# First norm of a two-layer hybrid trunk: the modulation of two channel tiles stands ahead of the row sums, the row sums read one tile for two, and the reciprocal square root starts from one operation

## The chip, the cores and the metric

One core of a Trainium2 chip runs the whole program in one launch. The metric is the device time in microseconds (us) of a run. Matrix products run on TensorE (PE, with its weight loads PEld), elementwise work on VectorE (DVE), activations and casts on ScalarE (ACT), masks on GpSimd (POOL). SyncE (SP) only issues transfers. What a profile shows is one execution; the three timed runs of the kernel before gave 1694.21, 1692.0 and 1687.25 us.

## The reference

Two layers act on 256 latent tokens and 256 context tokens of 1024 channels. Only what matters for this change is shown: the first thing a layer does is an RMS norm over the channels of each token, scaled and shifted per channel by a modulation (adaLN) that is a product of the conditioning vector with a weight matrix; then one wide input projection feeds four mixers.

```python
def rmsnorm(x, g):
    y = xf * lax.rsqrt(jnp.mean(xf * xf, axis=-1, keepdims=True) + EPS)
    return y.astype(x.dtype) * g

def modulate(h, shift, scale):
    return h * (1 + scale) + shift

def trunk_layer(xs, cs, c, c_ctx, p, rope_ret, rope_mla, last):
    mod_x = jnp.split((jax.nn.silu(c) @ p['w_ada'] + p['b_ada'])[:, None, :], 6, axis=-1)
    mod_c = jnp.split((jax.nn.silu(c_ctx) @ p['w_ada'] + p['b_ada'])[None, None, :], 6, axis=-1)
    hx = modulate(rmsnorm(xs, p['norm1_g']), mod_x[0], mod_x[1])
    hc = modulate(rmsnorm(cs, p['norm1_g']), mod_c[0], mod_c[1])
    mx, mc = token_mixers(hx, hc, p, rope_ret, rope_mla, not last)
    ...
```

## The kernel before

Channels lie on the 128 partitions, tokens along the free axis. The 1024 channels are eight tiles of 128 (`KD`), and a tile holds 512 tokens: 256 latent, then 256 context (the two streams). Each fp32 operand of the large products is split into a rounded part (hi) and a rest (lo), and one product is three matmuls: hi with hi, hi with lo, lo with hi (`mm3`). The weights of the projections come as one stream of chunks of 128 x 1024 (`raw`); ACT casts a chunk to its rounded part (`whi`, L168), DVE subtracts to get the rest (`wlo`, L230, two instructions of 512 columns). Three chunks can be held split, six unsplit.

The head of the program, which the change touches, goes as follows. SP issues the eight tiles of x, then `first_load(u)`, four transfers of 256 KB with the modulation weights of channel tile u, mixed with chunks of the projection. ACT squares the tiles of x, and `sq_add` sums the squares on DVE; it always leaves the last tile apart, so two tiles remain. `tok_sums` sums over the partitions with matmuls against a column of ones, one per 128 tokens and per tile that remains. `rsqrt` makes a first guess from the bits of the number and refines it, in nine small DVE operations. `bcast` spreads the result over the partitions with four transposes. `first_mod(u)` makes the modulation of channel tile u: 16 matmuls of 32 x 128 against `cs` (the conditioning vectors; 32 passes in the trace), a copy by ACT, one small matmul against `halves` (two passes in the trace), and two small DVE operations that write `mod` and `moda`. `norm_apply` then makes the normed tile u: DVE scales it (L226), ACT adds the shift and rounds (hi, L163), DVE takes the rest (lo, L226). Then the 18 matmuls of tile u go into six accumulators (`pre`) that stay open over all eight tiles.

The program is written as a sequence of calls. A scheduler then puts each engine's instructions into one fixed row, by its own estimates and priorities (`tc.high_priority` moves a piece ahead); at run time an engine takes its row in order and waits on semaphores. Another call order at the head, or one operation fewer, thus also changes rows far from it. In the mixers of a layer an interleaver (`interleave`) also chooses between the projections and the mixers by running totals of each engine's estimated time (`clk`), to which each `ts` or `tt` adds.

`rsqrt` is called 17 times: at the first norm, in the mixers of both layers, at the later norms and at the final one.

Of the kernel before, what the change touches and what calls it, by code (L numbers as in the profile page):

```python
# [13 lines left out]
I32 = mybir.dt.int32  # L14
AF = mybir.ActivationFunctionType
ALU = mybir.AluOpType
# [3 lines left out]
KD = D // 128  # L20
# [131 lines left out]
def trunk(ctx: ExitStack, tc: tile.TileContext, xin: bass.AP, cin: bass.AP, par: bass.AP, con: bass.AP,  # L152
# [47 lines left out]
    U = Slots(upool, NSLOT)  # L200
# [4 lines left out]
    def nm(s):  # L205
        cnt[0] += 1
        return f"{s}_{cnt[0]}"

    def mm():
        return psm.tile([128, 512], F32, tag="mm", name=nm("mm"))  # L210

    def mx():
        return psx.tile([128, 512], F32, tag="mx", name=nm("mx"))

    def sm(shape, tag, dtype=F32, bufs=2):
        return small.tile(shape, dtype, tag=tag, name=nm(tag), bufs=bufs)

    def width(o):
        n_ = 1
        for d_ in o.shape[1:]:  # L220
            n_ *= d_
        return n_

    def stt(o, i0, s, i1, op0, op1):
        clk["dve"] += 65 + 1.17 * width(o)
        V.scalar_tensor_tensor(out=o, in0=i0, scalar=s, in1=i1, op0=op0, op1=op1)  # L226

    def tt(o, i0, i1, op):
        clk["dve"] += 65 + 1.1 * width(o)
        V.tensor_tensor(out=o, in0=i0, in1=i1, op=op)  # L230

    def red(o, i, op):
        clk["dve"] += 65 + 1.15 * width(i)
        V.tensor_reduce(out=o, in_=i, axis=AX.X, op=op)

    def ts(o, i0, s1, op0, s2=None, op1=None):
        clk["dve"] += 65 + 0.8 * width(o)
        if op1 is None:
            V.tensor_scalar(out=o, in0=i0, scalar1=s1, scalar2=None, op0=op0)
        else:  # L240
            V.tensor_scalar(out=o, in0=i0, scalar1=s1, scalar2=s2, op0=op0, op1=op1)  # L241

    MUL, ADD, SUB, MAX = ALU.mult, ALU.add, ALU.subtract, ALU.max
# [10 lines left out]
    def mm3(o, ah, al, bh, bl, start, stop):  # L254
        clk["pe"] += 1.26 * width(o)
        PE.matmul(o, ah, bh, start=start, stop=False, skip_group_check=True)
        PE.matmul(o, ah, bl, start=False, stop=False, skip_group_check=True)
        PE.matmul(o, al, bh, start=False, stop=stop, skip_group_check=True)
# [81 lines left out]
    def w_load(chunk):  # L340
        while W["dma"] <= min(chunk, NCHUNK - 1):
            t = wpool.tile([128, 1024], F32, tag="raw", name=nm("raw"), bufs=NRAW)
            nc.sync.dma_start(t, wst[W["dma"]])
            W["raw"][W["dma"]] = t
            W["dma"] += 1
# [24 lines left out]
    def w_block(b, n=1):  # L370
        w_ensure(b // 8)
        hi, lo = W["hl"][b // 8]
        o = (b % 8) * 128
        return hi[:, o:o + 128 * n], lo[:, o:o + 128 * n]
# [110 lines left out]

    def rsqrt(v, shape):

        y, s, ti = sm(shape, "rs_y"), sm(shape, "rs_s"), sm(shape, "rs_i", I32)
        with tc.high_priority():
            ts(ti, v.bitcast(I32), 1, ALU.logical_shift_right)  # L490
            ts(y.bitcast(I32), ti, -1, MUL, 0x5F3759DF, ADD)

            tt(s, y, y, MUL)
            tt(s, s, v, MUL)
            stt(s, s, -10.0 / 3, s, ADD, MUL)
            stt(y, s, 5.0, y, ADD, MUL)
            stt(s, y, -0.5 * 0.375 ** 3, y, MUL, MUL)
            tt(s, s, v, MUL)
            stt(y, s, 1.5 * 0.375, y, ADD, MUL)
        return y  # L500

    def tok_sums(sums, N):

        nb = N // 128
        p = mx()
        for i, tiles in enumerate(sums):
            for b in range(nb):
                for j, t in enumerate(tiles):
                    PE.matmul(p[:, i * nb + b:i * nb + b + 1], t[:, b * 128:(b + 1) * 128], one, start=j == 0,
                              stop=j == len(tiles) - 1, skip_group_check=True)  # L510
        return p[:, 0:len(sums) * nb].rearrange("p (i b) -> p i b", b=nb)

    def rstd_of(sums, N, n, merge=True):
        shape = [128, len(sums), N // 128]
        if merge:
            r = sm(shape, "toks")
            for i, tiles in enumerate(sums):
                if len(tiles) == 2:
                    t = tiles.pop()
                    tt(tiles[0][:, :N], tiles[0][:, :N], t[:, :N], ADD)  # L520
                    U.put(t)
                p = mx()
                for b in range(N // 128):
                    PE.transpose(p[:, b * 128:(b + 1) * 128], tiles[0][:, b * 128:(b + 1) * 128], ident)
                red(r[:, i, :], p[:, :N].rearrange("p (b t) -> p b t", t=128), ADD)
            ts(r, r, 1.0 / n, MUL, EPS, ADD)
            return rsqrt(r, shape)
        r = sm(shape, "toks")
        ts(r, tok_sums(sums, N), 1.0 / n, MUL, EPS, ADD)
        return rsqrt(r, shape)  # L530

    def bcast(r, N):

        p = mx()
        for b in range(N // 128):
            PE.transpose(p[:, b * 128:(b + 1) * 128], r[:, b:b + 1].to_broadcast([128, 128]), ident)
        return p

    def sq_add(acc, src, N):

        t = U([128, N])
        A.activation(t[:, :N], src, AF.Square)
        acc = acc or []
        if len(acc) < 2:
            return acc + [t]
        tt(acc[0][:, :N], acc[0][:, :N], acc[1][:, :N], ADD)
        U.put(acc[1])
        return [acc[0], t]
# [13 lines left out]
    def norm_apply(hx, src, s, rb, ab, only=None, r0=0):  # L562

        c = slice(s * SEQ, (s + 1) * SEQ)
        for k in range(KD) if only is None else [only]:
            y = U([128, SEQ])
            hi, lo = hx[k]
            b = ab[1][:, k, s:s + 1]
            stt(y, src[k][:, c], ab[0][:, k, s:s + 1], rb[:, r0:r0 + SEQ], MUL, MUL)
            A.activation(hi[:, c], y, AF.Identity, bias=b)  # L570
            stt(lo[:, c], y, b, hi[:, c].bitcast(F32), ADD, SUB)
            U.put(y)
# [47 lines left out]
    def first_load(u):  # L620
        if u < KD:
            ada_tiles[u] = [U([128, 512]) for _ in range(4)]
            for i_, t_ in enumerate(ada_tiles[u]):
                nc.sync.dma_start(t_, wfirst[u, i_])
# [3 lines left out]
    def first_mod(u):  # L628

        p = mx()  # L630
        for k in range(KD):
            for h in range(2):
                j = h + 2 * (k % 2)
                PE.matmul(p[32 * j:32 * j + 32, 0:128], cs[:, k, :],
                          ada_tiles[u][k // 2][:, (2 * (k % 2) + h) * 128:(2 * (k % 2) + h + 1) * 128], start=k < 2,
                          stop=k >= KD - 2, tile_position=(0, 32 * j), skip_group_check=True)
        U.put(ada_tiles.pop(u))
        sb = U([128, 128])
        A.copy(sb, p[:, 0:128])
        PE.matmul(p[:, 128:132], sb, halves, start=True, stop=True, skip_group_check=True)  # L640
        U.put(sb)
        o = PCOL["bada"][0]
        with tc.high_priority():
            tt(mods[0][:, u:u + 9:8, :], p[:, 128:132].rearrange("p (h s) -> p h s", h=2),
               params[0][:, o + u:o + u + 9:8].unsqueeze(2).to_broadcast([128, 2, 2]), ADD)
            stt(moda[:, u, :], mods[0][:, 8 + u, :], 1.0,
                params[0][:, PCOL["n1g"][0] + u:PCOL["n1g"][0] + u + 1].to_broadcast([128, 2]), ADD, MUL)
# [3 lines left out]
    first_load(1)  # L651
    w_load(1)
    first_load(2)
    nc.sync.dma_start(cons[:, nfirst:], con[:, nfirst:nres])
    acc = None
    for k in range(KD):
        acc = sq_add(acc, xs[k], T)
    rs = rstd_of([acc], T, D, False)
    U.put(acc)
    rb = bcast(rs[:, 0, :], T)  # L660
    hx = [None] * KD
    pre = [mm() for _ in range(4)] + [mx() for _ in range(2)]
    pos = w_take([(("w_in", 0), k, cols) for k in range(KD)
                  for cols in [misc_cols] + [ar(OFF["xbc"] + 128 * c) for c in FIRST]])
    W["ahead"], W["load"] = 0, 1
    began = clk["pe"]
    first_mod(0)
    for u in range(KD):
        hx[u] = U.pair(T)
        for s in range(2):  # L670
            norm_apply(hx, xs, s, rb, (moda, mods[0][:, 0:8, :]), u, s * SEQ)
        if u + 1 < KD:
            first_mod(u + 1)
        for i, ps in enumerate(pre):
            wh, wl = w_block(pos + 6 * u + i)
            mm3(ps, wh, wl, hx[u][0], hx[u][1], u == 0, u == KD - 1)
        first_load(u + 3)
    W["ahead"], W["load"] = AHEAD, NLOAD
    U.put(xs)
    for c0 in range(2048, 6144, 1024):  # L680
# [2 lines left out]
    for l in range(L):  # L683
# [817 lines left out]
        if last:  # L1501
            acc = r
# [11 lines left out]
    for b in range(2):  # L1514
        for h in range(2):
            p, y = mm(), U([128, 512])
# [132 lines left out]
```

## Time and profile before

| | |
|---|---|
| median of three runs | 1692.0 us (1687.25 to 1694.21) |
| the profiled execution's own time | 1692.55 us |
| its span on the core | 1690.8 us |
| PE busy | 1641.8 us, 97% of the span |
| DVE busy | 1312.9 us, 78% |
| ACT busy | 812.0 us, 48% |
| bytes moved | 259.04 MB, 153 GB/s over the span |

Busy shares are means over stages with different limits. PE's matmuls are pipelined, so its busy time also holds time in which it is slowed by its clock or by weight loads. Times of rows are counted from the start of the span.

### The profile page before, as it was taken

What the parts mean: (1) busy time and instruction counts of PE and PEld (TensorE: products, weight loads), DVE (VectorE), ACT (ScalarE), POOL (GpSimd) and SP (SyncE); (2) the same over time, 40 slices, a digit from 0 to 9 for tenths busy, and PEclk for the clock granted to TensorE, in tenths of its full rate; (3) what the DMA queues carried; (4) which work ended last, traced back from release to release, by engine and by line L of the source; (5) the groups of instructions that cost most, each with busy time, mean ns of one, the idle gap of its engine ahead of it and who ended that gap; (6) DMA issues with size and microseconds to landing.
All of it is one profiled execution on the core that took longest, in us unless ns stands there. A gap on an engine that the chain in (4) does not pass through costs nothing.

```text
span 1690.8 us, 24270 instructions
## 1 busy us (share of the span) xinstructions
PE 1641.8 (97%) x8926; PEld 1359.7 (80%) x8926; DVE 1312.9 (78%) x2676; ACT 812.0 (48%) x1378; POOL 53.5 (3%) x89
## 2 busy tenths in 40 slices
PE   6999999999999999999999999999999999999998
PEld 4777766778888888988888889978778788778887
DVE  4779999988578568887666757699889967887765
ACT  3475759462234233522212235457577545455654
POOL 0020200000000000000000000001110000000000
PEclk9999999999999999999999999999999999999999
DMA  9353321214445445465456646445433377646664
GB/s 362 122 145 113 114 68 54 75 38 131 157 126 185 130 157 187 128 196 165 148 174 190 228 146 203 143 126 164 123 100 101 100 221 244 211 152 189 185 188 141
DMA packets 85096, 259.04 MB, mean 153 GB/s; under 512 B 9648, under 2 KB 18784, under 8 KB 84976
## 3 DMA queue, kind: packets, MB, share of 16 engines
q1 hardware_dynamic: 73584, 244.15, 45.8%
q10 hardware_dynamic: 10624, 12.28, 2.9%
q0 software_dynamic: 768, 1.05, 0.3%
q8 instruction: 70, 1.15, 0.3%
q14 instruction: 50, 0.41, 0.1%
HBM read 253.70 MB, written 2.18 MB: 151 GB/s over the span
## 4 chain that ended last, share of the span: by engine, by line
PE 86%; DVE 5%; DMA 4%; ACT 3%; issue 1%; POOL 0%; ACTq 0%; DVEq 0%; SPq 0%
PE mm L187 74%; PE mx L187 9%; DMA u<-drow 3%; PE mx L191 2%; DVE u L226 2%; ACT u L163 2%; DVE wlo L230 1%; DVE u L230 1%; ACT whi L168 1%; ACT u L168 1%; DVE u L241 0%; DMA u<-u 0%; DMA u<-xin 0%; DMA raw<-w_ada 0%; DMA drow<-u 0%
## 5 line engine op out<-in xcount | busy, mean ns | idle before, releaser
L187 PE MATMUL mm<-u,whi 128*128 128x512 f32 (+1 forms) x4088 | 1149.6, 362 | 3.7 <-DVE u L226 1.8
L187 PEld LDWEIGHTS mm<-u,whi 128*128 128x128 f32 x4088 | 728.1, 189 | 130.5 <-issue 12.1
L187 PE MATMUL mm<-u,wlo 128*128 128x256 f32 (+1 forms) x2332 | 785.3, 337 | 0.0
L168 ACT CAST whi<-raw 128x1024 fp32r<-128x1024 f32 x351 | 368.4, 1050 | 548.7 <-PE mm L187 328.8
L230 DVE TENSOR_TENSOR wlo<-raw,whi 128x512 fp32r<-128x512 f32 x702 | 461.7, 688 | 165.7 <-ACT whi L168 164.4
L187 PEld LDWEIGHTS mm<-u,wlo 128*128 128x128 f32 x2332 | 441.8, 189 | 47.0 <-issue 2.0
L226 DVE SCALAR_TENSOR_TENSOR u<-raw,cs,u 128x512 f32<-128x512 f32 x210 | 148.2, 746 | 80.7 <-DMA raw<-w_ada 80.6
L163 ACT ACTIVATE u<-u 128x256 f32<-128x256 f32 (+5 forms) x262 | 122.7, 484 | 150.5 <-DVE u L230 105.8
L187 PE MATMUL mm<-whi,u 128*128 128x512 f32 x544 | 172.7, 394 | 0.5 <-ACT u L163 0.5
L230 DVE TENSOR_TENSOR u<-u,u 128x256 f32<-128x256 f32 (+5 forms) x290 | 160.3, 571 | 8.3 <-ACT u L163 3.2
L187 PE MATMUL mx<-u,u 128*64 128x256 f32 (+6 forms) x644 | 132.1, 396 | 12.3 <-ACT whi L168 3.8
L226 DVE SCALAR_TENSOR_TENSOR u<-u,convw,u 128x510 f32<-128x510 f32 (+29 forms) x240 | 134.0, 599 | 0.0
L187 PEld LDWEIGHTS mx<-u,u 128*64 128x64 f32 (+3 forms) x644 | 79.8, 165 | 54.3 <-issue 13.5
L187 PEld LDWEIGHTS mm<-whi,u 128*128 128x128 f32 x544 | 101.8, 188 | 23.3 <-issue 1.7
L187 PE MATMUL mm<-wlo,u 128*128 128x512 f32 x272 | 106.4, 391 | 0.0
L163 ACT ACTIVATE u<-mm 128x512 f32<-128x512 f32 (+3 forms) x110 | 60.6, 553 | 40.1 <-PE mm L187 35.7
L226 DVE SCALAR_TENSOR_TENSOR u<-u,mm 128x512 f32<-128x512 f32 (+1 forms) x94 | 60.0, 647 | 19.8 <-PE mm L187 18.2
L226 DVE SCALAR_TENSOR_TENSOR u<-u,u 128x256 fp32r<-128x256 f32 (+3 forms) x113 | 61.0, 550 | 10.3 <-ACT u L163 10.3
L187 PEld LDWEIGHTS mm<-wlo,u 128*128 128x128 f32 x272 | 51.1, 188 | 10.7 <-issue 0.4
L168 ACT COPY u<-mx 128x512 f32<-128x512 f32 (+4 forms) x82 | 38.5, 495 | 38.1 <-PE mx L187 36.4
L191 PE MATMUL mx<-cons,u 128*128 128x128 f32 (+1 forms) x292 | 44.1, 276 | 4.8 <-DVE u L230 3.1
L1056 POOL TENSOR_SCALAR_AFFINE_SELECT u<-u 128x256 f32<-128x256 f32 x24 | 17.4, 726 | 983.2 <-DVE u L241 825.5
(116 smaller groups left out, 890.3 us busy)
## 6 DMA issues: line engine op xcount, KB each, us to landing
raw<-wst SPq DMA_DIRECT2D x354, 512.0 KB, 3.7
raw<-w_ada SPq DMA_DIRECT2D x72, 512.0 KB, 4.1
u<-wfirst SPq DMA_DIRECT2D x32, 256.0 KB, 6.0
u<-drow ACTq DMA_DIRECT2D x32, 256.0 KB, 4.7
u<-xin SPq DMA_DIRECT2D x16, 256.0 KB, 4.3
u<-w_ada SPq DMA_DIRECT2D x16, 256.0 KB, 5.3
u<-drow ACTq DMA_DIRECT2D x16, 128.0 KB, 3.9
spill<-u SPq DMA_DIRECT2D x8, 128.0 KB, 3.6
```

Source lines behind the costliest of these rows:

```text
L163: nc.scalar.activation(o, *a, **k)
L168: nc.scalar.copy(o, i)
L187: PE._place(nc.tensor.matmul(*a, **k))
L191: PE._place(nc.tensor.transpose(*a, **k))
L226: V.scalar_tensor_tensor(out=o, in0=i0, scalar=s, in1=i1, op0=op0, op1=op1)
L230: V.tensor_tensor(out=o, in0=i0, in1=i1, op=op)
L1056: G.affine_select(out=a_[:, 0:4:3], in_=a_[:, 0:4:3], pattern=[[0, 2], [1, 128]], compare_op=ALU.is_ge, fill=-1e5, base=0, channel_multipl ...
```

## The change

Three edits. `rsqrt` makes its first guess in one DVE operation: the integer bits are multiplied by -0.5 and the magic constant is added, where there had been a shift and then a multiply by -1 with the addition. At the first norm the two remaining tiles of squares are added by DVE, so that the ones matmuls read one tile. And the modulation runs ahead: `first_mod(0)` stands before that addition and the sums, `first_mod(1)` behind the broadcast, and in the loop `first_mod(u + 2)` stands behind the matmuls of tile u, where `first_mod(u + 1)` had stood before them; the loads are issued one tile earlier to match.

```diff
     def rsqrt(v, shape):
 
-        y, s, ti = sm(shape, "rs_y"), sm(shape, "rs_s"), sm(shape, "rs_i", I32)
+        y, s = sm(shape, "rs_y"), sm(shape, "rs_s")
         with tc.high_priority():
-            ts(ti, v.bitcast(I32), 1, ALU.logical_shift_right)
-            ts(y.bitcast(I32), ti, -1, MUL, 0x5F3759DF, ADD)
+            ts(y.bitcast(I32), v.bitcast(I32), -0.5, MUL, 0x5F3759DF, ADD)
...
     first_load(2)
+    first_load(3)
     nc.sync.dma_start(cons[:, nfirst:], con[:, nfirst:nres])
     acc = None
     for k in range(KD):
         acc = sq_add(acc, xs[k], T)
+    first_mod(0)
+    tt(acc[0], acc[0], acc[1], ADD)
+    U.put(acc.pop())
     rs = rstd_of([acc], T, D, False)
     U.put(acc)
     rb = bcast(rs[:, 0, :], T)
+    first_mod(1)
...
     began = clk["pe"]
-    first_mod(0)
     for u in range(KD):
         hx[u] = U.pair(T)
         for s in range(2):
             norm_apply(hx, xs, s, rb, (moda, mods[0][:, 0:8, :]), u, s * SEQ)
-        if u + 1 < KD:
-            first_mod(u + 1)
         for i, ps in enumerate(pre):
             wh, wl = w_block(pos + 6 * u + i)
             mm3(ps, wh, wl, hx[u][0], hx[u][1], u == 0, u == KD - 1)
-        first_load(u + 3)
+        if u + 2 < KD:
+            first_mod(u + 2)
+        first_load(u + 4)
```

Place 1, the start of PE's row. `one` marks the row sums, `rs_y` the broadcast, `cs` the modulation matmuls (a row of four is a quarter of a tile's modulation), `cons` with size 128x4 the small matmul against `halves`, `mm_` and `whi` the projection. Before, where `mx_203` is the modulation of tile 0 and `mx_235` that of tile 1:

```order
L187 MATMUL mx_170<-one,u_147 128x1
L187 MATMUL mx_170<-one,u_166 128x1
L191 MATMUL mx_192<-cons,rs_y_180 128x128 x4
L187 MATMUL mx_203<-u_118,cs 32x128 x4
L187 MATMUL mx_203<-u_119,cs 32x128 x4
L187 MATMUL mx_203<-u_120,cs 32x128 x4
L187 MATMUL mx_203<-u_121,cs 32x128 x4
L187 MATMUL mx_235<-u_128,cs 32x128 x4
L187 MATMUL mx_203<-cons,u_220 128x4
```

The same place of the changed kernel, with `mx_177` for tile 0, `mx_222` for tile 1 and `u_250` for the first normed tile:

```order
L187 MATMUL mx_177<-u_118,cs 32x128 x4
L187 MATMUL mx_177<-u_119,cs 32x128 x4
L187 MATMUL mx_201<-one,u_155 128x1 x4
L187 MATMUL mx_177<-u_120,cs 32x128 x4
L187 MATMUL mx_177<-u_121,cs 32x128 x4
L191 MATMUL mx_217<-cons,rs_y_207 128x128 x2
L187 MATMUL mx_177<-cons,u_194 128x4
L191 MATMUL mx_217<-cons,rs_y_207 128x128 x2
L187 MATMUL mx_222<-u_128,cs 32x128 x4
L187 MATMUL mx_222<-u_129,cs 32x128 x4
L187 MATMUL mm_244<-u_250,whi_260 128x512
```

The modulation of tile 0 moved ahead of the sums (one half) and under the reciprocal root (the other half); the second half of tile 1's, which stood wholly ahead of the first projection matmul, now stands among those.

Place 2, in PE's row, where the modulation of channel tile 4 is made. Before (`mx_428`), at the border of two tiles, with `u_418` and `u_419` the hi and lo of the next one:

```order
L187 MATMUL mx_428<-u_345,cs 32x128 x4
L187 MATMUL mx_428<-u_346,cs 32x128 x4
L187 MATMUL mx_428<-u_347,cs 32x128 x4
L187 MATMUL mx_428<-u_348,cs 32x128 x4
L187 MATMUL mm_197<-u_418,whi_399 128x512
L187 MATMUL mm_197<-u_419,whi_399 128x512
L187 MATMUL mx_428<-cons,u_445 128x4
L187 MATMUL mm_197<-u_418,wlo_400 128x512
```

In the changed kernel (`mx_413` is tile 4, `mx_471` tile 5), inside tile 2's matmuls:

```order
L187 MATMUL mx_413<-u_308,cs 32x128 x4
L187 MATMUL mx_413<-cons,u_430 128x4
L187 MATMUL mx_471<-u_370,cs 32x128 x3
L187 MATMUL mx_248<-u_378,whi_402 128x512
L187 MATMUL mx_248<-u_379,whi_402 128x512
L187 MATMUL mx_249<-u_378,whi_402 128x512
L187 MATMUL mx_249<-u_379,whi_402 128x512
L187 MATMUL mx_248<-u_378,wlo_403 128x512
L187 MATMUL mx_249<-u_378,wlo_403 128x512
```

The small matmul now stands directly behind the modulation that feeds it through ACT, with no projection matmul between. On ACT the cast of `whi_402` stands directly behind the copy for that small matmul, and on DVE `wlo_403` stands behind the small operations of tile 4 and its two scalings.

Place 3, in DVE's row, at the modulation of tile 7 (`mx_608` before, `mx_593` after). Before:

```order
L226 SCALAR_TENSOR_TENSOR u_599<-u_604,mod_115,u_598 128x256
L230 TENSOR_TENSOR wlo_645<-raw_579,whi_644 128x512 x2
L230 TENSOR_TENSOR wlo_841<-raw_642,whi_840 128x512 x2
L230 TENSOR_TENSOR mod_115<-mx_608,par_99 128x2x2
L226 SCALAR_TENSOR_TENSOR moda_117<-mod_115,par_99 128x2
L226 SCALAR_TENSOR_TENSOR u_657<-u_93,moda_117,mx_192 128x256
L226 SCALAR_TENSOR_TENSOR u_661<-u_93,moda_117,mx_192 128x256
```

In the changed kernel (`u_617` and `u_621` scale the two streams of tile 6, `u_652` and `u_656` those of tile 7):

```order
L226 SCALAR_TENSOR_TENSOR u_617<-u_91,moda_117,mx_217 128x256
L230 TENSOR_TENSOR wlo_640<-raw_574,whi_639 128x512 x2
L226 SCALAR_TENSOR_TENSOR u_616<-u_617,mod_115,u_615 128x256
L230 TENSOR_TENSOR wlo_836<-raw_637,whi_835 128x512 x2
L230 TENSOR_TENSOR mod_115<-mx_593,par_99 128x2x2
L226 SCALAR_TENSOR_TENSOR u_621<-u_91,moda_117,mx_217 128x256
L226 SCALAR_TENSOR_TENSOR moda_117<-mod_115,par_99 128x2
L226 SCALAR_TENSOR_TENSOR u_652<-u_93,moda_117,mx_217 128x256
```

The scaling of tile 6's second stream moved behind the operation that waits for tile 7's modulation; in PE's row the first projection matmul of tile 6 stands right behind that modulation and its small matmul.

## Rows read from the trace of the kernel before

**Rows 1.** The page: engines' busy time, and the chain that ended last.
```profile
PE 1641.8 (97%) x8926; PEld 1359.7 (80%) x8926; DVE 1312.9 (78%) x2676; ACT 812.0 (48%) x1378; POOL 53.5 (3%) x89
...
PE 86%; DVE 5%; DMA 4%; ACT 3%; issue 1%; POOL 0%; ACTq 0%; DVEq 0%; SPq 0%
```

**Rows 2.** Busy time by stretch: PE, PEld, DVE, ACT, POOL, clock, DMA share, GB/s.
```profile
0.00:30.70 30.70, 13.86 (x106) 11.67 (x106) 13.41 (x48) 10.91 (x22) 0.77 (x9) 0.94 0.96 349
30.70:75.00 44.30, 44.30 (x364) 34.62 (x363) 28.54 (x67) 19.00 (x34) 0.00 (x0) 1.00 0.57 202
```

**Rows 3.** Timeline of PE, 13 to 25 us: start, duration, instruction, idle before.
```profile
13.07 3.55 PE L187 MATMUL mx<-one,u 128*128 128x1 f32 x16 [13.07 <-DVE u L230]
18.66 1.11 PE L191 MATMUL mx<-cons,rs_y 128*128 128x128 f32 x4 [2.04 <-DVE rs_y L226]
...
24.79 0.66 PE L187 MATMUL mm<-u,whi 128*128 128x512 f32 x1 [1.59 <-ACT u L163]
```

**Rows 4.** Timeline of the head, DVE.
```profile
12.23 0.69 DVE L230 TENSOR_TENSOR u<-u,u 128x512 f32<-128x512 f32 x1
...
16.66 0.16 DVE L241 TENSOR_SCALAR toks<-mx 128x4 f32<-128x4 f32 x1 [3.73 <-PE mx L187]
16.85 0.17 DVE L239 TENSOR_SCALAR rs_i<-toks 128x4 int32<-128x4 int32 x1
...
22.52 0.68 DVE L230 TENSOR_TENSOR wlo<-raw,whi 128x512 fp32r<-128x512 f32 x1
...
23.31 0.87 DVE L226 SCALAR_TENSOR_TENSOR u<-u,moda,mx 128x256 f32<-128x256 f32 x2
```

**Rows 5.** Issues of tile 0's modulation weights; landing times, issues of 0 to 60 us.
```profile
6.76 2.36 SPq L624 DMA_DIRECT2D u<-wfirst  x4
...
u<-wfirst SPq DMA_DIRECT2D x32, 256.0 KB, 6.0
raw<-wst SPq DMA_DIRECT2D x12, 512.0 KB, 6.6
```

**Rows 6.** Timeline at the border of channel tiles 0 and 1; a later chunk's split.
```profile
30.60 0.39 PE L187 MATMUL mx<-u,wlo 128*128 128x512 f32 x1
30.92 0.81 PEld L187 LDWEIGHTS mx<-u,cs 128*32 128x32 f32 x32 [0.35 <-issue]
...
31.93 0.73 PE L187 MATMUL mm<-u,whi 128*128 128x512 f32 x2
32.07 0.27 ACT L168 COPY u<-mx 128x128 f32<-128x128 f32 x1 [4.55 <-PE mx L187]
32.38 0.31 PEld L187 LDWEIGHTS mx<-cons,u 128*128 128x128 f32 x2 [0.16 <-ACT u L168]
...
32.64 0.48 PE L187 MATMUL mm<-u,wlo 128*128 128x512 f32 x1
...
33.21 0.87 DVE L226 SCALAR_TENSOR_TENSOR u<-u,moda,mx 128x256 f32<-128x256 f32 x2
...
37.78 1.05 ACT L168 CAST whi<-raw 128x1024 fp32r<-128x1024 f32 x1
...
39.55 1.29 DVE L230 TENSOR_TENSOR wlo<-raw,whi 128x512 fp32r<-128x512 f32 x2
```

**Rows 7.** Chain that ended last: start, duration, piece: ten projection matmuls.
```profile
32.78 2.40 PE mm L187 x10
```

**Rows 8.** Busy time and clock of one microsecond after the first projection matmul.
```profile
25.00:26.00 1.00, 1.00 (x4) 0.98 (x4) 0.51 (x3) 0.83 (x1) 0.00 (x0) 0.50 1.04 399
```

**Rows 9.** PE's waits for the reciprocal root: total, times, longest; and the last root.
```profile
PE mx L191 <- DVE rs_y L226: 6.0, 7, 2.0
...
1683.00 0.18 DVE rs_i L239
```

**Rows 10.** The longest wait of PE behind the head, and its stretch.
```profile
1203.76 1.08 PE L187 MATMUL mx<-u,u 128*64 128x256 f32 x2 [3.83 <-ACT whi L168]
...
1200.00:1210.00 10.00, 6.24 (x17) 4.51 (x18) 8.19 (x19) 4.77 (x11) 3.33 (x3) 0.66 0.29 103
```

## Prediction

> **What bounds the kernel now.** I read the page first: PE is busy 97% of the span, and 86% of the chain that ended last lies on it [rows 1]. So a change pays where PE waits or where its work gets shorter. The table by stretches shows one large place: in the first 30.7 us PE is busy only 13.9, and from 30.7 to 75 us it has no idle time at all [rows 2]. The head is therefore where a wait can go, and behind it anything put between PE's matmuls costs its full time. The timeline of the head shows the chain: the last sum of squares on DVE starts at 12.23, the ones matmuls run from 13.07, DVE reads their result at 16.66, the broadcast starts at 18.66, the first normed tile is scaled at 23.31 and the first projection matmul starts at 24.79 [rows 3, 4].
>
> **What the change removes, at the first matmul.** One more addition of 0.69 us on DVE [rows 4] puts the sums to 13.76. Half of 16 passes go, at 3.55 / 16 = 0.222 each [rows 3]: 1.78 us. One operation of the root goes; its step is 16.85 - 16.66 = 0.19 [rows 4]. The broadcast then starts at 18.66 + 0.69 - 1.78 - 0.19 = 17.38. It takes 1.11 [rows 3]. The small matmul of tile 0 stands inside it and costs what it costs at a tile border: from 31.93 to 32.64 PE does two projection matmuls and it [rows 6], and ten projection matmuls take 2.40, so 0.24 each [rows 7]; 0.71 - 0.48 = 0.23. The broadcast is done at 18.72, where it had been done at 19.77. Before, the scaling came 3.54 us behind it: the modulation of tile 0, its copy, its two small operations, and half a weight split of 0.68 at 22.52 [rows 4] stood between. Now the modulation runs ahead of the sums and under the root, and the split stands behind the scaling, so the scaling starts at about 18.75. That is 4.56 us earlier, and the first projection matmul comes at 20.23 instead of 24.79.
>
> The transfers allow it. The four issues of tile 0's weights end at 9.12, and a landing takes 6.0 in the median: 15.1 at the latest, before the sums end at 13.76 + 1.78 = 15.5 [rows 5]; half of them aren't waited for by the sums at all. The chunk that tile 2 first needs is now issued behind four more transfers. With it, 8 x 256 KB of x, 20 x 256 KB of modulation weights, 832 KB of constants, 3 x 512 KB of the projection and some 0.4 MB of parameters have to come, about 10.2 MB, which at the head's 349 GB/s [rows 2] is 29 us; a landing of such a chunk takes 6.6 in the median [rows 5], most of it the same queueing. By the sums below, tile 2 needs it after 33 us. I cost the changed order of SP at 0; if that cover were gone, it would cost the 3 us that the extra 1 MB takes, once.
>
> **What PE pays back, up to its 75th microsecond.** Three terms.
>
> (a) The modulation matmuls lie less well. A whole group of 32 passes lies between the matmul at 30.60 and the one at 31.93 [rows 6]: 1.33 - 0.24 = 1.09, of which 0.81 are its weight loads, 0.025 per pass, and 0.28 the change of shape in and out. Before, tile 1's group ran while PE waited, and six groups lay between projection matmuls. Now half of tile 1's passes lie there too, 16 x 0.025 = 0.40. Tile 1's second half lies in two pieces, tile 2's group in three, tile 5's in two (one of them at tile 4's), so there are ten changes of shape instead of six: 4 x 0.28 = 1.12. Sum 1.5; from 0.4, if a change of shape costs nothing among these, to 2.3, if the first two pieces run at the half clock and take twice as long.
>
> (b) At tile 4's modulation the small matmul stands directly behind it. Take T for PE's next free slot, 31.93 in the rows. The copy runs from T + 0.14 to T + 0.41, and PE is past the small matmul at T + 0.71 [rows 6]; before, projection matmuls covered that and it cost 0.23. Behind it ACT casts the chunk which the next matmuls need, 1.05 [rows 6], to T + 1.46. Behind the scaling, which starts at T + 1.28 and takes 0.87, DVE splits it, in two halves of 0.65 [rows 6], to T + 2.80 or T + 3.44. PE does a piece of tile 5 and four matmuls meanwhile, 0.23 + 0.38 + 0.96 = 1.57 without a wait, and then needs that split: it loses 1.2, or 1.9 if it needs both halves. I take 1.2, since the next block lies in the first half; 0 if tile 2 already lags behind.
>
> (c) At tile 7's modulation the second stream of tile 6 is scaled only behind the operation that waits for tile 7's small matmul. The scaling starts at T + 1.28 less one small step, T + 1.1, and takes 0.44 for one stream. From the scaling at 23.31 to the first matmul at 24.79 it took 1.48 with two streams [rows 3, 4], so 0.61 beyond them. PE goes on at T + 2.1 instead of T + 0.23: 1.9. It is 0 only if an engine did not keep to its row.
>
> On (b) and (c) the rows of before show what a row's order means: the load for the small matmul waits 0.16 at 32.38, and the projection matmul behind it, whose data had long been there, starts only at 32.64 [rows 6]. The Trainium skill ("TensorE: Matmul & The Clock Gate", Part 2) states that "the MATMULs themselves stay in program order" and that only weight loads are pulled ahead. By that rule (b) and (c) are paid in full; were it otherwise, the sum would be that of the second rival.
>
> The head thus gains 4.56 and pays 1.5 + 1.2 + 1.9 = 4.6: nothing is left, 0.0.
>
> **The other sixteen roots.** The last one lies bare at the end, its first operation at 1683.00 [rows 9]: 0.19. PE waited for a root seven times, 6.0 in all, 2.04 of them at the first [rows 3, 9]; the other six can lose 0.19 each, 1.1, or nothing where DVE does other work between the steps. I take 0.5.
>
> **Sum.** 1692.55, the profiled execution's own time, 0.0 for the head, - 0.2, - 0.5: 1691.85. That execution stands 0.55 above the median of the runs, so 1691.3. Bounds: with nothing paid back and all six waits shortened, 1692.0 - 4.56 - 0.2 - 1.1 = 1686.1; with the upper ends 2.3 + 1.9 + 1.9 = 6.1 and no shorter wait, 1692.0 + 1.5 - 0.2 = 1693.3.
>
> **Rivals.**
>
> First, the clock. Tile 0 took from 24.79 to 30.84, 6.05 us, where 18 matmuls and a small one are 4.56 [rows 3, 6, 7]: 1.5 lost, while PE ran at a granted 0.50 (1.2 GHz), having waited 1.59 just before [rows 3, 8]. If PE, with less waiting ahead of tile 0, keeps 2.4 GHz there, the time is 1689.8. For it: PE now works through most of 13.7 to 19.5. Against: it still waits some 0.9 before the first matmul, for the scaling and its rounding. The same page, Part 1, says that the window of this gate is free-running and doesn't reset at a kernel's start; by that the 1.5 would come and go from run to run in both kernels. No row of one execution shows it.
>
> Second, the early start is kept: the pieces hide in waits, and the engines' real times at (b) and (c) leave no wait. 1692.0 - 4.56 - 0.7 = 1686.7. For it: DVE and ACT have much idle time from 30.7 to 75 us [rows 2]. Against: their rows are fixed, and the waits follow from the rows, not from load.
>
> Third, slower: a new wait in a mixer. The scheduler put PE's, ACT's and DVE's rows of both layers' mixers in another order at many places. Where a cast of weights comes to stand on ACT behind an operation that waits for a transfer, PE runs out of split weights. The longest such wait of before is 3.83 us, and its stretch of 10 us ran at 0.66 of the clock [rows 10], so 6.8 us at half speed and at most 3.4 lost besides: 7.2. One more of these gives 1698.5. It decides as soon as it is over 0.7, and needs ACT to wait longer than the split chunks held ahead last. For it: such waits are there. Against: the interleaver's totals moved by only some 0.07 us per root, and most rows moved by a few places.
>
> Fourth, the same reordering takes that wait away: 1684.1.
>
> That the change does not do what it says, I can exclude for the order: the rows show it.
>
> **How the numbers follow.** Forecast, 45%: 1691.3, its own range 1688.5 to 1694. Clock 10%, 1689.8. Early start kept 20%, 1686.7. New wait 14%, 1698.5 or, with two, beyond 1700. A wait gone 11%, 1684.1 or, with the early start kept, below 1683. The range 1684.5 to 1698.5 leaves out half of each of the last two cases and a little of the rest. 0.5%, 8.5 us, is about what a measurement of this kernel can tell from no change: that is below 1683.5 or above 1700.5. Only two cases together reach the first, 0.11; only two new waits, or one with a longer shadow, the second, 0.08; 0.81 remain.
>
> **What would show it.** Right: sums of eight passes that end near 15.5; the first projection matmul near 20.2; waits of PE at the small matmuls of tiles 4 and 7, about 0.5 and then 0.7 or more, and about 1.4 at tile 7; the end of tile 7's matmuls within a microsecond of before; eight operations per root. Wrong: no wait at these two places and an end of tile 7 some 3 us or more earlier (the second rival); tile 0's matmuls 0.24 apart from the start (the first); or a wait of PE over 2 us in a mixer that before doesn't have, or one less (the third and fourth). Most of all the prediction would be wrong if the mixers moved by more than the head.

## The result: 0.6% slower, by a loss in the head and a larger one in the mixers

Before: 1691.18 us median (5 runs, 1687.25 to 1694.21). After: 1699.74 us (5 runs, 1698.39 to 1700.98). Ratio 1.006, interval 1.0044 to 1.0075: 8.6 us slower by the medians, where I had forecast no change. The profiled execution of after took 1700.98 us, its span 1699.0.

The head by stretches, as in [rows 2] (PE, PEld, DVE, ACT, POOL, clock, DMA share, GB/s): PE is busy 3 us more up to 30.7 us, and idle for 2.4 in the stretch behind it, where before had no idle time.

```profile
0.00:30.70 30.70, 16.84 (x114) 10.96 (x114) 13.93 (x48) 10.81 (x22) 0.77 (x9) 1.00 0.97 352
30.70:75.00 44.30, 41.93 (x329) 31.44 (x325) 23.26 (x55) 17.41 (x31) 0.00 (x0) 0.96 0.52 188
```

The root and the scaling on DVE, as in [rows 4]:

```profile
15.74 0.16 DVE L241 TENSOR_SCALAR toks<-mx 128x4 f32<-128x4 f32 x1 [1.96 <-PE mx L187]
...
19.01 0.87 DVE L226 SCALAR_TENSOR_TENSOR u<-u,moda,mx 128x256 f32<-128x256 f32 x2 [0.17 <-PE mx L191]
```

PE's timeline of after from the sums to the end of tile 7, as in [rows 3]: start, duration, instruction, idle time before it.

```profile
13.84 1.86 PE L187 MATMUL mx<-one,u 128*128 128x1 f32 x8 [0.67 <-DVE u L230]
...
17.54 0.69 PE L191 MATMUL mx<-cons,rs_y 128*128 128x128 f32 x2 [0.83 <-DVE rs_y L226]
...
20.49 1.65 PE L187 MATMUL mm<-u,whi 128*128 128x512 f32 x3 [0.51 <-ACT u L163]
...
26.69 0.63 PE L187 MATMUL mm<-u,whi 128*128 128x512 f32 x1
27.12 0.63 PE L187 MATMUL mm<-u,wlo 128*128 128x512 f32 x1
...
30.17 0.65 PE L187 MATMUL mx<-u,cs 128*32 128x128 f32 x16
...
42.10 0.39 PE L187 MATMUL mx<-cons,u 128*128 128x4 f32 x2 [0.39 <-ACT u L168]
42.74 0.42 PE L187 MATMUL mx<-u,cs 128*32 128x128 f32 x6 [0.26 <-DVE mod L230]
44.45 0.73 PE L187 MATMUL mx<-u,wlo 128*128 128x512 f32 x2 [0.16 <-DVE wlo L230]
...
61.76 0.39 PE L187 MATMUL mx<-cons,u 128*128 128x4 f32 x2 [0.39 <-ACT u L168]
63.33 0.98 PE L187 MATMUL mm<-u,whi 128*128 128x512 f32 x2 [1.18 <-ACT u L163]
...
73.31 0.41 PE L191 MATMUL mx<-cons,u 16*128 16x16 f32 x4
```

The last row is the first matmul behind the head; I call it the end marker. In before it is

```profile
68.28 0.42 PE L191 MATMUL mx<-cons,u 16*128 16x16 f32 x4
```

So the first projection matmul comes 4.30 us earlier (20.49 for 24.79), and the end marker 5.03 later: 9.33 were paid back. Tile 0 takes from 20.49 to 30.17, 9.68, where it took 24.79 to 30.92, 6.13; its matmuls are 0.43 apart up to 29.25. That is the spacing of before's stretch with a granted 0.50 [rows 8]; the profile of after has no clock record before 29.5, so the clock of 1.00 in its first stretch above was not measured there. Behind tile 0 comes 43.14 where before had 37.36. Of these 5.78, five rows show 0.39 + 0.26 + 0.16 + 0.39 + 1.18 = 2.38 of idle time, and the clock fell once behind the last of them.

The mixers: from 170 to 210 us PE does 9 us less work than before, and part of it at half the clock. First before, then after:

```profile
170.00:210.00 40.00, 38.55 (x192) 27.79 (x191) 38.17 (x82) 28.58 (x65) 9.38 (x15) 1.00 0.39 117
```

```profile
170.00:210.00 40.00, 29.42 (x139) 19.07 (x140) 36.29 (x80) 25.22 (x60) 12.78 (x16) 0.87 0.33 102
210.00:380.00 170.00, 169.64 (x805) 127.53 (x805) 160.81 (x309) 110.39 (x218) 5.46 (x8) 1.00 0.21 65
```

The waits in it, in PE's timeline of after:

```profile
186.56 1.98 PE L187 MATMUL mx<-u,u 128*64 128x256 f32 x8 [3.08 <-DVE u L230]
...
198.84 0.73 PE L187 MATMUL mm<-u,whi 128*128 128x512 f32 x2 [2.75 <-ACT u L168]
203.23 0.66 PE L191 MATMUL mx<-cons,u 128*128 128x128 f32 x2 [2.57 <-DVE u L230]
```

Before has none over 0.84 there. From 210 to 380 us after is the fuller one (169.64 for 165.56 busy), so 4.1 of the 9 us of work are made good there.

### The profile page after: what moved, and what is told of

Read it like the earlier page. It is cut to its first block, busy times and chain, and to the rows that moved or that the text cites. A ratio compares the mean times of both kernels' runs of the same rounds, so it can differ in the third digit from the quotient of the medians.

```text
span 1699.0 us, 24229 instructions
## 1 busy us (share of the span) xinstructions
PE 1649.1 (97%) x8918; PEld 1362.5 (80%) x8918; DVE 1311.5 (77%) x2660; ACT 811.4 (48%) x1378; POOL 55.7 (3%) x89
## 4 chain that ended last, share of the span: by engine, by line
PE 89%; DMA 5%; DVE 2%; ACT 2%; issue 1%; SPq 0%; ACTq 0%; POOL 0%; DVEq 0%
PE mm L187 77%; PE mx L187 9%; PE mx L191 2%; DMA u<-drow 2%; DMA u<-wfirst 1%; DMA raw<-wst 1%; ACT whi L168 1%; DVE wlo L230 1%; ACT u L163 1%; DVE u L230 1%; DVE u L226 1%; DVE u L241 0%; DMA par<-par 0%; ACT u L168 0%; DMA u<-u 0%
## 5 line engine op out<-in xcount | busy, mean ns | idle before, releaser
L168 ACT COPY u<-mm 128x256 f32<-128x256 f32 (+2 forms) x98 | 45.1, 464 | 8.7 <-PE mm L187 8.2
```

Of the source, the lines that this page charges most:

```text
L168: nc.scalar.copy(o, i)
```

## The experiments

All times are medians against runs of before on the same chip (1690.47, 1691.37 and 1691.11 us for E1 to E4, E5 to E8, E9 to E12). The last two columns: the end marker, and PE's busy time and clock from 170 to 210 us, in the profiled execution. A ratio is not the quotient of the two medians (for E2 that would be 1.0025); a loss in us of E1, E2, E4 and E8 below is what the ratio is over 1, times 1691.

| | Edit | Median us | Ratio, interval | Marker | 170:210 |
|---|---|---|---|---|---|
| - | before | 1691.18 | | 68.28 | 38.55, 1.00 |
| - | after | 1699.74 | 1.0060 (1.0044-1.0075) | 73.31 | 29.42, 0.87 |
| E1 | root alone | 1697.35 | 1.0037 (1.0023-1.0051) | 68.36 | 30.36, 0.79 |
| E2 | head alone | 1694.63 | 1.0016 (1.0001-1.0031) | 71.68 | 38.47, 1.00 |
| E3 | after + 6 idle matmuls | 1701.00 | 1.0052 (1.0035-1.0070) | 70.81 | 30.93, 0.79 |
| E4 | before + 6 idle matmuls | 1694.08 | 1.0016 (1.0002-1.0029) | 68.54 | 38.49, 1.00 |
| E5 | E2, PE's row by hand | 1691.49 | 1.0007 (0.9992-1.0022) | 68.65 | 39.24, 1.00 |
| E6 | E5 + 14 idle matmuls, row tied from the start | 1691.18 | 0.9995 (0.9980-1.0010) | 67.25 | 38.77, 1.00 |
| E7 | root, old account | 1691.81 | 1.0001 (0.9987-1.0015) | 68.73 | 37.49, 1.00 |
| E8 | account alone | 1696.85 | 1.0036 (1.0021-1.0051) | 68.77 | 31.66, 0.83 |
| E9 | E5, DVE and ACT by hand | 1688.93 | 0.9984 (0.9972-0.9997) | 67.29 | 38.52, 1.00 |
| E10 | E9 + 10 idle matmuls, broadcast tied too | 1691.08 | 0.9993 (0.9980-1.0006) | 69.10 | 38.46, 1.00 |
| E11 | E10 + root, old account | 1691.80 | 0.9997 (0.9982-1.0012) | 67.72 | 37.88, 1.00 |
| E12 | after, old account | 1692.87 | 1.0005 (0.9990-1.0020) | 70.71 | 37.56, 1.00 |

**The change in its two halves.** E1 is before with the new root; E2 is after with the old one.

```diff
# E1, on before                     # E2, on after: the reverse
...
-  ts(ti, v.bitcast(I32), 1, ALU.logical_shift_right)
-  ts(y.bitcast(I32), ti, -1, MUL, 0x5F3759DF, ADD)
+  ts(y.bitcast(I32), v.bitcast(I32), -0.5, MUL, 0x5F3759DF, ADD)
```

E1: 

> The kernel before with the root's first guess in one operation, and nothing else of the change; the head's rows stay as before, the mixers' rows are those of the changed kernel. Theory (two parts that add up: head +5, the mixers' new order +4): head as before, its end marker at 68.3 within 0.5 us; then layer 0 loses about 3.9 us between its markers at 157 and 374 us, the rest within 1 us; time 1691.2 + 3.5 = 1694.7. Rival 1 (the mixers lose because the head ends later and at another phase, not because of their order): mixers as before or shorter by some tenths, 1690.7. Rival 2 (all of the loss is the mixers'): 1699.

E2: 

> The changed kernel with the old root of two operations: the head's rows are those of the changed kernel, the mixers' rows those of before. Theory: first projection matmul near 20.7, tile 0's matmuls 0.43 us apart to about 29.5, waits of PE near 0.4 and 1.2 us at tile 7's modulation, head's end marker at 73 instead of 68.3; then no further loss: 1691.2 + 4.9 = 1696.1. Rival 1 (the head's shift makes the mixers lose too): 1699.5. Rival 2 (the head's +5 is an accident of the clock in one execution and not of the order): 1692.

E1 is 6.3 us slower (0.37%), E2 2.7 (0.16%, from 0.2 to 5.2 by its interval); together 9.0, and both at once cost 8.6 by the medians and 10 by the ratio. E1's head is before's, and its stretch from 170 to 210 us is like after's. E2 has it the other way round, and in its head the two waits of tile 7 stand again:

```profile
60.06 0.39 PE L187 MATMUL mx<-cons,u 128*128 128x4 f32 x2 [0.39 <-ACT u L168]
61.62 1.21 PE L187 MATMUL mm<-u,whi 128*128 128x512 f32 x4 [1.18 <-ACT u L163]
```

So neither half is the cause alone (the head's part is the less certain one, see E12), and the mixers' loss does not need the head's shift. I had expected E1 2.65 lower and E2 1.5 higher.

**What of the root makes the mixers slower.** An operation fewer shortens DVE's work; but it also takes 65 + 0.8 x width ns, some 0.07 us, off the planner's total for DVE, by which it puts a mixer's step ahead of the next projection matmuls as soon as that total (or the mixers' own, which grows with it) plus a lookahead is below PE's total (line 595 of before, in `interleave`). E7 takes the operation away and keeps the total; E8 keeps the operation and changes the total alone.

```diff
# E7, on E1, behind the one operation
+  clk["dve"] += 65 + 0.8 * width(y)
# E8, on before, behind the two operations
+  clk["dve"] -= 65 + 0.8 * width(y)
# E12, on after: as E7
```

E7: 

> The kernel before with the one-operation guess, while the planner that interleaves the mixers still counts two operations per root: the order of the program's text is as before, and what is left of the reordering comes from the scheduler alone. Theory A (the planner's totals moved the mixers' pieces and made the waits between 180 and 204 us): these waits go back to under 3 us in sum, time 1690.5 - 0.5 = 1690. Theory B (the scheduler's own reordering by the shorter root made them): 9 us of waits there and 1697 as with the root alone.

E8: 

> The mirror of the run before: the two-operation guess of before, while the planner counts one operation per root. No instruction is removed. Theory A (planner's totals): the waits between 180 and 204 us appear, 8 us or more, and the time is near 1697 though no operation was changed. Theory B (scheduler and the shorter root): as before, 1690.5.

E12: 

> The changed kernel, all of it, while the planner still counts two operations per root. Theory (head +2.7, planner's totals +6, independent of each other): the mixers' loss goes and the head's stays, 1691.2 + 2.7 - 0.5 = 1693.4, head's end marker at 71 to 73.3. Rival (the loss in the mixers comes back with this head): 1697 to 1700.

E7 is at 1.0001, E8 at 1.0036: the whole loss of E1, with every operation of before still in it. Theory A stands. PE's timeline shows what was moved: before has projection matmuls (`mm` rows) between three pieces of a mixer (`u,u`),

```profile
176.95 2.06 PE L187 MATMUL mx<-u,u 128*128 128x256 f32 x15
178.84 0.63 PE L187 MATMUL mm<-u,whi 128*128 128x512 f32 x2
179.40 0.65 PE L187 MATMUL mx<-u,u 128*64 128x256 f32 x2
...
182.15 0.39 PE L187 MATMUL mm<-u,wlo 128*128 128x512 f32 x1
182.47 1.08 PE L187 MATMUL mx<-u,u 128*64 128x256 f32 x8
```

and in E8 these three stand next to each other, at nearly the same times, so PE waits for DVE instead of projecting:

```profile
177.26 2.05 PE L187 MATMUL mx<-u,u 128*128 128x256 f32 x15 [0.64 <-DVE u L230]
179.66 0.65 PE L187 MATMUL mx<-u,u 128*64 128x256 f32 x2 [0.35 <-DVE u L230]
182.62 1.78 PE L187 MATMUL mx<-u,u 128*64 128x256 f32 x8 [2.31 <-DVE u L230]
...
195.33 1.22 PE L187 MATMUL mm<-u,whi 128*128 128x512 f32 x2 [3.14 <-ACT u L168]
```

The projection matmuls are done later: from 210 to 380 us E8's PE is busy 169.83 where before's was 165.56, so of the 6.9 us of work missing from 170 to 210 only 4.3 fall into idle time there. And PE ran at a mean clock of 0.83 over those 40 us, which makes the waits dearer than their idle time. E12, after with the old total, is at 1692.87, 0.5 below what was expected: its marker shows the head's loss, its stretch from 170 to 210 us that the mixers' is gone. Its ratio is only 0.8 us above before (-1.7 to 3.4), with E2's head but for the root: so the head costs between nothing and some 5 us by these two, and that it costs anything rests on E2's interval and on the markers, which come later in all four profiled executions of this head.

**The clock in tile 0.** E3 and E4 put six matmuls on zeros in front of all work.

```diff
+    warm = U([128, 512])
+    G.memset(warm, 0.0)
+    wp = mx()
+    for _ in range(6):
+        PE.matmul(wp, warm[:, 0:128], warm, start=True, stop=True, skip_group_check=True)
+    U.put(warm)
```

E3: 

> The changed kernel with six matmuls on a tile of zeros (128x512) on PE ahead of everything else, written to a PSUM tile that nobody reads; all other rows stand as in the changed kernel. Theory (tile 0 ran at 1.2 GHz because PE had done only thin work before it): tile 0's matmuls come 0.24 instead of 0.43 us apart, the 18 of them end 18 x 0.19 = 3.4 us earlier at most, and the eight passes of the sums get shorter as well; the end of tile 7 comes 3 us earlier, time 1699.7 - 3.0 = 1696.7, unless tile 7's wait and the clock's fall behind it stay where transfers set them. Rival (0.43 us is what the weights' split or their transfer allows): spacing stays 0.43 and the time 1699.7 within 1.

E4: 

> The kernel before with the same six matmuls on zeros ahead of all work, every other row as before. Theory: tile 0's matmuls are 0.24 apart from 24.8 on, where they were 0.43 apart to 28.3: 8 x 0.19 = 1.5 us, and the sums and the modulation ahead of it are shorter by up to 1.5: time 1691.2 - 1.5 to - 3.0, 1689.0. Rival (spacing set by the split weights): 1691.2.

Neither paid. In E3 the six end near 9.5 us, PE then waits 2.19 for data, and tile 0 runs at the lower clock again until 27 us. Behind tile 0, though, E3 shows what the fall at tile 7 is worth: all its other rows stand as in after, its clock stays at 1.00 from 60 to 75 us, and from the group of tile 7 to the marker it takes 11.42, where after, with 0.86 and 0.79 in two stretches of 5 us from 60 us on, takes 13.01 (60.30 to 73.31): 1.6.

```profile
59.39 1.08 PE L187 MATMUL mx<-u,cs 128*32 128x128 f32 x32
...
70.81 0.42 PE L191 MATMUL mx<-cons,u 16*128 16x16 f32 x4
```

In E4 the sums get faster (16 passes in 1.95 us instead of 3.55) and the root starts 1.67 earlier, but only 0.34 is left at the first projection matmul. The head's rows did not stay those of before, which I had taken for granted: on DVE the whole weight split, 1.29 us, now stands between the scalings of tile 0's two streams, which had stood together [rows 4], so the second one starts only at 23.38, where in before the pair ran from 23.31 to 24.18, and the matmul, which reads both streams, waits for it through ACT. E4 therefore does not price the sums' clock.

```profile
21.78 1.29 DVE L230 TENSOR_TENSOR wlo<-raw,whi 128x512 fp32r<-128x512 f32 x2
...
23.38 0.47 DVE L226 SCALAR_TENSOR_TENSOR u<-u,moda,mx 128x256 f32<-128x256 f32 x1
...
24.45 0.80 PE L187 MATMUL mm<-u,whi 128*128 128x512 f32 x1 [1.63 <-ACT u L163]
```

That E4 is 2.7 us above before by its ratio I can't explain: its marker is only 0.26 later, and its profiled execution, 1689.75, was its fastest.

**Can the early start be kept?** E5 ties PE's row of the head to an order written out: two blocks of projection, the next tile's small matmul, two blocks, the whole modulation group of the tile after it. E9 does the same for DVE and ACT, and puts the small matmul of tile 7 two blocks earlier. E6 and E10 add idle matmuls on zeros and tie more of PE's row (E6 from its first instruction, E10 the root and the broadcast), E11 adds the root as in E7.

```diff
# E5, on E2
+            if i == 2 and u + 1 < KD:
+                first_small(u + 1)
+            if i == 4 and u + 2 < KD:
+                first_group(u + 2)
             mm3(ps, wh, wl, hx[u][0], hx[u][1], u == 0, u == KD - 1)
-        if u + 2 < KD:
-            first_mod(u + 2)
# E9, on E5: behind first_small(u + 1)
+                normed(u + 1)
+            if i == 3 and u + 1 < KD:
+                w_ensure((pos + 6 * u + 11) // 8)
```

E5: 

> The head of the changed kernel (two tiles' modulation ahead, half as many sums) with the old root, and with PE's instructions in the head tied to an order written out by hand: the small matmul of the next tile behind two blocks of projection matmuls, the whole modulation group of the tile after that behind two more blocks. Mixers as before. Theory (the early start is lost to the row order: the small matmuls of tiles 4 and 7 wait, the modulation is cut in pieces): no wait of PE from tile 1 to tile 7, groups of 32 passes whole, first projection matmul near 20.8; from there to the head's end marker as long as before, 43.5 us, plus 0 to 2 us for a tile 0 that runs at 1.2 GHz: marker at 64.3 to 66.3 instead of 68.3, time 1690.5 - 3 = 1687.5. Rival (the weights' transfers or the clock hold the head whatever the order): marker at 68 or later, 1690.5 to 1693.

E6: 

> As the chained head, with 14 matmuls on a tile of zeros, result unread: 11 ahead of all work, two between the sums and the broadcast, one ahead of the first projection matmul, so that PE has little idle time from 1.8 us to tile 0. Theory of the clock: tile 0's matmuls are 0.24 us apart from the start and the eight passes of the sums take about 1 us instead of 1.9, head's end marker at 62 to 63.5, time 1690.5 - 6 = 1684.5. Rival (PE's clock falls in the head whatever PE did just before): marker as in the chained head, 64.3 to 66.3, 1687.5. Second rival (tile 0's modulation waits for its weights to land, near 12.5 us or later, and the filled gaps only delay the chain): first projection matmul at 21 or later, 1688.

E9: 

> The chained head once more (old root, mixers as before), now with DVE's and ACT's instructions of the head tied to the program's order too, the next tile's norm written right behind its small matmul, the split of the next tile's weights behind that norm, and tile 7's small matmul two blocks earlier. Theory (what the chained head still lost were waits for a cast or a norm that stood late in ACT's and DVE's rows, three of them, 0.34, 0.51 and 0.81 us, about 2.2 with the restart behind each): no wait from tile 1 to tile 7, head's end marker at 66.4, the rest of the early start lost to tile 0 at 1.2 GHz; time 1691.4 - 2.2 = 1689.2. Rival (transfers of the weights set these waits): marker 68.6 again, 1691.4.

E10: 

> As the run before, with ten matmuls on zeros, result unread: nine ahead of all work, one between the sums and the broadcast. Theory (the clock takes the rest): tile 0 at 0.24 apart from its start, first projection matmul at 20 to 20.8, head's end marker at 64 to 65; time 1691.4 - 4 = 1687.4. Rival (the clock falls before tile 0 all the same, since PE idles again ahead of the sums): marker 66.4, 1689.2.

E11: 

> As the run before, with the one-operation guess in all roots while the planner still counts two. Theory (the guess itself is worth 0.2 to 1 us, its loss came from the planner's totals alone): 0.5 us below the run before, waits between 180 and 204 us under 3 us; 1686.9, the fastest of all. Rival (any change of the roots reorders the mixers to their loss): 1690 or more.

E5 removes the waits at the small matmuls, but not the loss: its marker is at 68.65, where its rival had it. Three other waits appear, not for transfers but for a cast and for norms that stand late in ACT's and DVE's rows.

```profile
39.23 0.73 PE L187 MATMUL mx<-u,whi 128*128 128x512 f32 x2 [0.34 <-ACT whi L168]
...
58.33 1.02 PE L187 MATMUL mm<-u,whi 128*128 128x512 f32 x2 [0.51 <-ACT u L163]
...
64.57 0.50 PE L187 MATMUL mm<-u,whi 128*128 128x512 f32 x1 [0.81 <-DVE u L226]
```

E9 takes the first two away and makes one of its own, at the small matmul that I moved:

```profile
57.25 0.39 PE L197 MATMUL mx<-cons,u 128*128 128x4 f32 x2 [0.93 <-ACT u L178]
63.21 0.50 PE L197 MATMUL mm<-u,whi 128*128 128x512 f32 x1 [0.83 <-DVE u L236]
67.29 0.42 PE L201 MATMUL mx<-cons,u 16*128 16x16 f32 x4
```

Its marker is 1 us earlier than before's, not the 1.9 expected, and its time 0.16% below before: the only kernel whose interval lies on the fast side of 1, by 0.0003, among twelve tried, so that one such case may be chance. Both kernels are beaten by it, before only just if at all. The idle matmuls bought nothing that can be measured: E6's tile 0 runs at the full clock from its second row, but in its tied row the small matmul of tile 0 stands ahead of the sums and waits 2.05 for ACT's copy, the sums start at 17.08 instead of 13.69 (E5), and the first projection matmul at 22.32; E9's tile 0, with no idle matmul, is at the full clock from its second row too; E10's tile 0 starts at half the clock although PE had done ten of them; its marker is later than E9's. E11's root is worth nothing next to E10, and brings back no wait: the expected 0.5 is below what these runs can tell.

## Why the prediction was wrong

**What held.** The working up to the first projection matmul: sums from 13.84 (13.76), result read at 15.74 (15.5), broadcast 17.54 (17.38), scaling 19.01 (18.75), first matmul 20.49 (20.23); 4.30 gained of 4.56. The waits (b) and (c) are at the small matmuls of tiles 4 and 7, where the rows put them: 0.81 and 1.57 idle. So PE does keep to its row, as the Trainium skill ("TensorE: Matmul & The Clock Gate", Part 2), cited there, has it, and the second rival falls.

The three terms of what PE pays back came out within half a microsecond of their sizes. These rows are the groups of modulation matmuls of before, then of after, by which the time behind tile 0 can be split, and tile 0 of E12, whose head has the rows of after, engine by engine:

```profile
36.47 1.08 PE L187 MATMUL mx<-u,cs 128*32 128x128 f32 x32
53.11 1.08 PE L187 MATMUL mx<-u,cs 128*32 128x128 f32 x32
58.65 1.08 PE L187 MATMUL mx<-u,cs 128*32 128x128 f32 x32
```

```profile
36.42 1.08 PE L187 MATMUL mx<-u,cs 128*32 128x128 f32 x32
54.74 1.08 PE L187 MATMUL mx<-u,cs 128*32 128x128 f32 x32
60.30 1.08 PE L187 MATMUL mx<-u,cs 128*32 128x128 f32 x32
```

```profile
20.46 1.65 PE L187 MATMUL mm<-u,whi 128*128 128x512 f32 x3 [0.50 <-ACT u L163]
27.55 0.64 PE L187 MATMUL mx<-u,cs 128*32 128x128 f32 x16
```

| Term | Where it is read | Forecast us | Measured us |
|---|---|---|---|
| (a) pieces | tile 0 in E12, 7.09 for 6.13, at about as long a half clock as in before; group of tile 2 to that of tile 3, 6.25 for 5.55 | 1.5 | 0.96 + 0.70 = 1.66 |
| (b) tile 4 | group of tile 3 to that of tile 6, 18.32 for 16.64 | 1.2 | 1.68 |
| (c) tile 7 | group of tile 7 to the marker at the full clock (E3), 11.42 for 9.63 | 1.9 | 1.79 |
| the clock behind (c) | the same in after, 13.01 for 11.42 | none | 1.59 |
| the clock in tile 0 | 9.68 (after) for 7.09 (E12) | none | 0 to 2.59 |

**The first step that failed: the head's net of 0.0, by the clock that was put at nothing.** Gained 4.30, paid 5.1 by (a) to (c): the marker would be 0.8 later. It is 2.4 (E12) to 5.0 (after) later in four profiled executions; in time it is +2.7 by E2's ratio and +0.8 by E12's, each with some 2.5 either way. What the sum left out are the two prices of the clock: 1.6 behind the wait of tile 7, in all of these executions but E3's, and up to 2.6 in tile 0. The prediction had a rival for the clock, but in one direction only, that tile 0 might run faster. The clock rose at 28.4 in before, at 24.1 in E12 and at 29.3 in after: tile 0, which starts 4.3 us earlier, ran at half the clock for some 3.6 us in before and E12 and for 8.8 in after.

**The second step that failed: the mixers taken as they were.** "The interleaver's totals moved by only some 0.07 us per root" was true and was the wrong measure. The planner compares totals, and a small shift moves a whole piece past a block of projection. That change of order cost 6 us (E8), thirty times the 0.19 that a root's shorter chain can give at the end. The third rival, at 14%, named the loss and its size (7.2), with a cast on ACT as its place; the place was another, PE waiting for DVE (E8: 2.31) and then for ACT (3.14). How many rows had moved could not have told: E7's rows, too, stand in another order than before's at many places of the mixers, and it costs nothing. What counts is which piece moves, and the prediction names none.

**The sum.** Head +2.7 and mixers +6.1 (E2, E8) make 1700.0 from 1691.2; measured 1699.74, outside the range that I had given. That it fits so closely is partly luck, as each term has some 2.5 us either way; with E12 in place of E2 it is 1698.1. The roots' own gain (forecast 0.7) isn't seen: E7 is at 1.0001, with 2.4 us either way, though all waits of PE for a root go from 6.0 [rows 9] to 5.3 in it.

## What to carry to other kernels

Where a planner counts costs, an edit has two effects, on the work and on the plan; try each alone, the edit with the old count and the count without the edit, before judging either. An earlier start is kept only if every row behind it has cover: follow each engine's row to the next full stretch, and price the slow clock behind each wait as well. One profiled execution places a loss, and even a dozen runs leave 0.15% either way here, so a loss of 0.2% wants two experiments that agree.

## What the runs showed of the hardware

The same rows met different clocks. After and E12 have the same head, row for row on PE, DVE and ACT; tile 0's matmuls go from 0.43 to 0.23 apart at 29.3 us in one and at 24.1 in the other, and the group of tile 2 starts at 30.17 and 27.55. These are the same eight modulation passes in after and in E12, and what E12 does next:

```profile
23.80 0.66 PE L187 MATMUL mx<-u,cs 128*32 128x128 f32 x8
```

```profile
23.77 0.43 PE L187 MATMUL mx<-u,cs 128*32 128x128 f32 x8
...
25.38 0.40 PE L187 MATMUL mm<-u,whi 128*128 128x512 f32 x1
25.61 0.40 PE L187 MATMUL mm<-u,wlo 128*128 128x512 f32 x1
```

E5 and E9 differ in the same way: up to the middle of tile 0 they have the same row on PE, and the third matmul of tile 0 runs at half the clock in E5 and at the full clock in E9, neither of which has an idle matmul:

```profile
22.58 0.63 PE L187 MATMUL mm<-u,wlo 128*128 128x512 f32 x1
```

```profile
22.86 0.39 PE L197 MATMUL mm<-u,wlo 128*128 128x512 f32 x1
```

So one execution can't show whether idle matmuls ahead of the work raise the clock in tile 0.

The Trainium skill ("TensorE: Matmul & The Clock Gate", Part 1) says that the gate's window is free-running and does not reset when a kernel starts; the executions of after and E12 agree. I had cited that rule and still counted tile 0's 1.5 as fixed. Before itself spread over 1684.4 to 1699.6 us in 35 runs, as far as the whole effect and more; how much of that is this clock no run here shows.
